# A long convolution placed beside a recurrence: one pair of heads and 128 channels at a time

## The chip, the cores and the metric

The kernel runs on one core of one Trainium2 chip. The metric is device time in microseconds (us); where several runs are shown, their median. The names in the profile: PE is TensorE (PEld its weight loads), DVE is VectorE, ACT is ScalarE, POOL is GpSimd, SP is SyncE, which here only issues transfers.

## The reference, cut to what matters

The model is two blocks. The first has an attention layer and a recurrent layer, the second another set of attention and recurrent branches and a feed-forward part. The change is in the recurrent layer of the first block, between its input product and its output product. There two branches are independent of each other: a linear recurrence of 8 heads over 256 context and 1024 latent tokens in both directions, and a long convolution of 512 channels, applied twice with a gate, by Fourier transforms of length 2048.

```python
def wkv_scan(s0, r, decay, k, v, kk, b, reverse, emit):
    def step(s, inp):
        r_t, w_t, k_t, v_t, kk_t, b_t = inp
        sa = jnp.einsum('bhij,bhj->bhi', s, kk_t)
        s = s * w_t[:, :, None, :] - sa[..., None] * b_t[:, :, None, :] + v_t[..., None] * k_t[:, :, None, :]
        y = jnp.einsum('bhij,bhj->bhi', s, r_t) if emit else None
        return s, y
    ...

def hyena_operator(u, short_taps, kern, skip):
    v, x1, x2 = split_cols(centred_conv3(u, short_taps), (HY_WIDTH, HY_WIDTH, HY_WIDTH))
    z = v
    for o, gate in enumerate((x1, x2)):
        z = gate * fft_long_conv(z, kern[:, o], skip[o])
    return z

def rec_layer(...):
    ...
    y_rw, yc_rw = rwkv_branch(u_rw, uc_rw, ...)
    y_hy = hyena_operator(u_hy, hy_short, hyena_filters(...), hy_skip)
    y = jnp.concatenate([y_rw * jax.nn.silu(g_rw), y_hy * jax.nn.silu(g_hy)], axis=-1) @ w_out
```

## The kernel before, in words

The program is written as Python generators that issue instructions; a scheduler of the tile framework then fixes the order of the instructions on each engine. At run time each engine takes its queue strictly in that order. PSUM has 8 banks; `banks(s=5, pt=2, o=1)` deals them out to tags, and `bank(tag)` goes round among the banks of a tag.

The recurrent layer's middle has these stages, one after the other:

- The input product (`rec_dense`), with the features of the recurrence and the triangular inverses (`rwkv_inverse`) of head pairs 0 and 1 and of the context as background work. An inverse is 31 rounds of a product (L1660, `ush`) and a subtraction (L1662, `r_X`).
- The convolution (`hyena`), alone. It goes through four passes, one for each order `o` and each half `hh` of 256 channels. A forward part transposes the input, multiplies it with the DFT table `F` (L1281, for each half `f` of the frequencies), and does the last butterflies and the product with the filter's spectrum `K` on VectorE (all through the helper at L1271). An inverse part multiplies the spectra `G` with the table `I` (L1338) and adds skip and gate on VectorE (L1342 and after it). `z` and `K` have two buffers, `G` three; the inverse of one pass is woven into the forward part of the next.
- The recurrence (`rwkv_chains`, `rwkv_scan`). Tokens are taken in chunks of 64: 4 chunks of context and 16 of latents, so 20 steps. A chain is one pair of heads in one direction. Four chains run at once, pairs 0 and 1 in 20 steps, then pairs 2 and 3 in 20 more. A step of a chain (`steps`): two matmuls with the state `SV` (L1789), a copy `R` on ScalarE (L1791), two matmuls (L1799), two copies into `UV`, one on ScalarE (L1800) and one on VectorE (L1801), two matmuls with `tm` (L1806), and two operations on VectorE that scale and add the state scaled before on GpSimd, `sp` (L1795), and so give the next `SV` (L1809). The output `y` (L1815, four matmuls) is copied on ScalarE (L1820) or added on VectorE (L1822). Every four steps each chain has one preparation (`prep`): `eta` on GpSimd (L1737), matmuls L1741, masks on VectorE (L1746), matmuls L1753 and the copy `tm` (L1755), copies of `SV` into `UV` (L1757), matmuls L1763 and copies `AE` (L1766), matmuls L1771 and copies `T` (L1774). Its seven loads go through SP's queue. Beside the first steps run the inverses of pairs 2 and 3, their products on GpSimd; beside steps 20 to 39 run the readouts of pairs 0 and 1.
- The output product (`rec_w_out`), which begins by splitting `yH` and `yB` on ScalarE (L406); the readouts of pairs 2 and 3 run beside its first part.

Of the kernel before, what the change touches and what calls it, by code (L numbers as in the profile page):

```python
# [11 lines left out]
F32 = mybir.dt.float32  # L12
# [1014 lines left out]
class KernB(Kern):  # L1027
# [198 lines left out]
    def hyena(self, d_hy, d_sgh, yH):  # L1226

        nc, tc, A = self.nc, self.tc, self.A
        self.banks(s=4, o=2, pt=2)
        with self.pool(name="hyF", bufs=1, side="right") as pf, self.pool(name="hy", bufs=1) as p:  # L1230
            F = self.t(pf, [128, 4, 1024], F32, "F")
            self.reserve(p, ("z", 8, 2), ("K", 8, 2), ("W1", 4, 1), ("W2", 4, 1), ("Z", 8, 1), ("T", 8, 1), ("Y", 8, 1), ("G", 8, 3))
            I = self.t(p, [128, 4, 1024], F32, "I")
            for r in range(4):
                nc.gpsimd.dma_start(yH[:, r], d_hy[r * 128:(r + 1) * 128, :])
                self.load_r(F[:, r], A["dft_f1"][r])
            inv = self.inverse_load(I)
            for o in range(2):
                for hh in range(2):
                    G = []  # L1240
                    for _ in self.hyena_fwd(p, o, hh, F, yH, G):
                        next(inv, None)
                    for _ in inv:
                        pass
                    inv = self.hyena_inv(p, o, hh, I, yH, G, d_hy, d_sgh)
            for _ in inv:
                pass
        self.banks(s=4, pt=2, o=2)

    def inverse_load(self, I):  # L1250

        for _ in range(4):
            yield
        for r in range(4):
            yield
            self.pace(self.load_r(I[:, r], self.A["dft_i1"][r]), self.mark)

    def hyena_fwd(self, p, o, hh, F, yH, Gs):

        nc = self.nc  # L1260
        z = self.t(p, [128, 8, 256], F32, "z", bufs=2)
        for cc in range(2):
            zr = yH[:, hh * 2 + cc].rearrange("p (t r) -> p r t", r=4)
            for q in range(2):
                ps = self.bank("o")
                for i in range(4):
                    j = q * 4 + i
                    nc.tensor.transpose(ps[:, i * 128:(i + 1) * 128], zr[:, j // 2, (j % 2) * 128:(j % 2) * 128 + 128], self.ident)
                nc.scalar.activation(z[:, q * 4:q * 4 + 4, cc * 128:(cc + 1) * 128], ps.rearrange("p (j c) -> p j c", c=128), AF.Copy)
                yield  # L1270
        add = lambda o, x, y, op=OP.add: nc.vector.tensor_tensor(o, x, y, op)  # L1271
        for f in range(2):
            K = self.t(p, [128, 4, 2, 256], F32, "K", bufs=2)
            nc.sync.dma_start(K.rearrange("p s c e -> p (s c e)"), self.d_spec[o, hh, f])
            X = {}
            for r in range(4):
                X[r] = self.bank("s", (128, 2, 256))
# [5 lines left out]
            E, O = (self.t(p, [128, 2, 2, 256], F32, n, bufs=1) for n in ("W1", "W2"))  # L1283
# [7 lines left out]
            Z = self.t(p, [128, 4, 2, 256], F32, "Z", bufs=1)  # L1291
# [3 lines left out]
            Y = self.t(p, [128, 4, 2, 256], F32, "Y", bufs=1)  # L1295
            T = self.t(p, [128, 4, 2, 256], F32, "T", bufs=1)
            part = lambda i: Z[:, :, i:i + 1].to_broadcast([128, 4, 2, 256])
# [11 lines left out]
            G = self.t(p, [128, 4, 2, 256], F32, "G", bufs=3)  # L1309
# [5 lines left out]
    def hyena_inv(self, p, o, hh, I, yH, Gs, d_hy, d_sgh):  # L1315

        nc = self.nc
        for cc in range(2):
            ct = hh * 2 + cc
            gate = self.t(p, [128, 1024], F32, "gate", bufs=2)  # L1320
            row = (1 + o) * 512 + ct * 128
            nc.sync.dma_start(gate, d_hy[row:row + 128, :])
            if o == 1:
                sg = self.t(p, [128, 1024], F32, "sgh", bufs=2)
                nc.sync.dma_start(sg, d_sgh[512 + ct * 128:512 + ct * 128 + 128, :])
                nc.vector.tensor_tensor(gate, gate, sg, OP.mult)
            zs = yH[:, ct]
            nc.scalar.activation(zs, zs, AF.Copy, scale=self.c("hy_skip", o * 4 + ct))
            zsr = zs.rearrange("p (t r) -> p r t", r=4)
            for rp in range(2):  # L1330
                ps = self.bank("pt", (128, 2, 256))
                for i in range(2):
                    r = rp * 2 + i
                    n = 0
                    for f in range(2):
                        for half in range(2):
# [346 lines left out]
    def rwkv_scan(self, p, R, yB, later):  # L1683
# [19 lines left out]
        for x in AEs:  # L1703
            nc.vector.memset(x, 0.0)
# [1047 lines left out]
```

## Time and profile before

| | us |
|---|---|
| median of 3 runs (lowest, highest) | 4325.55 (4324.6, 4327.83) |
| profiled execution | 4318.2 |
| its span | 4316.1 |
| its mean granted TensorE clock | 0.939 |
| busy in the span: PE | 3887.0 (90%) |
| DVE | 2779.1 (64%) |
| ACT | 1781.4 (41%) |
| POOL | 1357.6 (31%) |

The shares are averages over stages with different limits. What matters here is the stretch from 1858 us (end of the input product) to 2454 us (start of the output product). A matmul of fp32 data shows as two records, so 16 records of L1789 are one step of four chains. The clock column is the mean clock that TensorE was granted, as a share of 2.4 GHz.

### The profile page before, as it was taken

The numbers are of one execution on the slowest core, as the hardware profiler recorded it, in microseconds if no ns is written. First come the engines' busy times: TensorE is split into PE (matmuls) and PEld (weight loads), VectorE is DVE, ScalarE is ACT, GpSimd is POOL, SyncE is SP. The second block draws the span as 40 slices with busy tenths as digits, with TensorE's granted clock in tenths as the row PEclk, the third lists the DMA queues.
The fourth block names the chain that finished last, engine by engine and source line by source line (L and its number), as shares of the span: only waits on it lengthen the run. The fifth ranks groups of instructions, "written<-read, shape, count | busy, mean of one in ns | idle before, by whom it ended". The sixth has DMA issues, their size and how long they took to land.

```text
span 4316.1 us, 65300 instructions
## 1 busy us (share of the span) xinstructions
PE 3887.0 (90%) x23789; PEld 3168.0 (73%) x23789; DVE 2779.1 (64%) x5935; ACT 1781.4 (41%) x3746; POOL 1357.6 (31%) x1570
## 2 busy tenths in 40 slices
PE   7989998899999988977686888999997897999999
PEld 4768886777787767766675766777876785888787
DVE  7842426788844767759565656599777768656532
ACT  6433415777735544411453423334336523333311
POOL 5422302333324432300564334122212116554200
PEclk8899998999999999988897999999998998999999
DMA  5444326421234544531543323233336351222422
GB/s 209 151 168 164 130 75 168 122 70 31 78 109 127 184 143 135 170 144 67 134 124 107 111 65 115 93 105 116 122 105 172 105 185 58 88 79 83 151 102 74
DMA packets 351338, 511.29 MB, mean 118 GB/s; under 512 B 149864, under 2 KB 226424, under 8 KB 348329
## 3 DMA queue, kind: packets, MB, share of 16 engines
q1 hardware_dynamic: 332200, 436.33, 32.1%
q0 software_dynamic: 14064, 53.48, 3.6%
q10 hardware_dynamic: 4752, 17.30, 1.3%
q8 instruction: 188, 3.08, 0.3%
q14 instruction: 134, 1.09, 0.1%
HBM read 343.69 MB, written 164.63 MB: 118 GB/s over the span
## 4 chain that ended last, share of the span: by engine, by line
PE 37%; DVE 7%; DMA 2%; ACT 2%; issue 1%; POOL 1%; SPq 1%; ACTq 0%; DVEq 0%; POOLq 0%
PE bank L285 18%; PE bank L2493 10%; PE bank L2393 2%; DMA SV<-d_V 1%; PE bank L1741 1%; PE bank L1789 1%; PE bank L724 1%; PE bank L1815 1%; PE bank L1753 1%; PE bank L685 1%; PE bank L246 0%; DVE d L2225 0%; DVE S L694 0%; DVE SV L1809 0%; DVE junk L2225 0%
## 5 line engine op out<-in xcount | busy, mean ns | idle before, releaser
L285 PE MATMUL bank<-hhi,whi 128*128 128x512 f32 (+1 forms) x1264 | 488.6, 387 | 13.1 <-ACT hhi L399 10.1
L285 PE MATMUL bank<-hlo,whi 128*128 128x512 f32 (+1 forms) x1264 | 485.0, 384 | 4.3 <-DVE hlo L400 2.1
L285 PE MATMUL bank<-hhi,wlo 128*128 128x512 f32 (+1 forms) x1264 | 482.6, 382 | 0.0
L267 ACT ACTIVATE whi<-wf 128x1024 fp32r<-128x1024 f32 (+3 forms) x202 | 193.5, 960 | 462.1 <-PE bank L285 393.0
L268 POOL TENSOR_TENSOR wlo<-wf,whi 128x1024 fp32r<-128x1024 f32 (+1 forms) x96 | 220.5, 2298 | 462.9 <-ACT whi L267 427.8
L285 PEld LDWEIGHTS bank<-hhi,whi 128*128 128x128 f32 x1264 | 243.8, 193 | 62.7 <-ACT hhi L399 10.9
L285 PEld LDWEIGHTS bank<-hlo,whi 128*128 128x128 f32 x1264 | 243.7, 193 | 54.5 <-DVE hlo L400 4.6
L285 PEld LDWEIGHTS bank<-hhi,wlo 128*128 128x128 f32 x1264 | 242.9, 192 | 46.7
L2493 PE MATMUL bank<-th,wh 128*128 128x512 f32 x616 | 247.3, 402 | 6.8 <-ACT th L2418 6.8
L2493 PE MATMUL bank<-th,wl 128*128 128x512 f32 x616 | 246.6, 400 | 0.0
L411 POOL CAST phi<-split 128x512 fp32r<-128x512 f32 (+1 forms) x104 | 62.7, 603 | 476.4 <-ACT split L410 381.0
L322 POOL TENSOR_TENSOR walo<-wa,wahi 128x512 fp32r<-128x512 f32 x96 | 137.0, 1441 | 238.4 <-ACT wahi L321 224.0
L285 PE MATMUL bank<-yT,whi 128*128 128x512 f32 (+1 forms) x600 | 190.6, 387 | 1.1 <-ACT ush L1393 0.5
L407 DVE TENSOR_TENSOR plo<-bank,phi 128x512 fp32r<-128x512 f32 (+2 forms) x260 | 166.5, 653 | 34.9 <-ACT phi L406 32.6
L406 ACT ACTIVATE phi<-bank 128x512 fp32r<-128x512 f32 (+2 forms) x260 | 143.5, 563 | 66.7 <-PE bank L724 25.4
L1795 POOL TENSOR_SCALAR sp<-SV,PL 64x64 f32<-64x64 f32 x304 | 135.9, 448 | 80.9 <-DVE SV L1809 59.4
L285 PE MATMUL bank<-yH,whi 128*128 128x512 f32 x376 | 151.4, 403 | 7.9 <-ACT ev_a L2156 4.4
L285 PE MATMUL bank<-yB,whi 128*128 128x512 f32 x376 | 150.6, 401 | 8.0 <-DVE yB L397 7.2
L285 PE MATMUL bank<-yH,wlo 128*128 128x512 f32 x376 | 150.4, 400 | 0.0
L268 DVE TENSOR_TENSOR wlo<-wf,whi 128x1024 fp32r<-128x1024 f32 (+2 forms) x106 | 117.6, 1112 | 50.8 <-ACT whi L267 50.6
L2493 PE MATMUL bank<-tl,wh 128*128 128x512 f32 x352 | 141.8, 403 | 6.4 <-DVE tl L2419 5.2
L2493 PEld LDWEIGHTS bank<-th,wh 128*128 128x128 f32 x616 | 117.7, 191 | 36.7 <-ACT th L2418 8.7
(632 smaller groups left out, 11275.9 us busy)
## 6 DMA issues: line engine op xcount, KB each, us to landing
wf<-in_w_in_dram SPq DMA_DIRECT2D x47, 512.0 KB, 3.5
wf<-in_w_ffn_in_dram SPq DMA_DIRECT2D x44, 512.0 KB, 3.4
d_rec<-r_rec SPq DMA_DIRECT2D x40, 512.0 KB, 3.6
wf<-in_rec_w_in_dram ACTq DMA_DIRECT2D x33, 512.0 KB, 3.9
wf<-in_attn_w_in_dram SPq DMA_DIRECT2D x26, 512.0 KB, 4.3
wa<-in_attn_ada_w_dram POOLq DMA_DIRECT2D x24, 512.0 KB, 4.0
wa<-in_rec_ada_w_dram POOLq DMA_DIRECT2D x24, 512.0 KB, 4.2
LK<-d_rec SPq DMA_DIRECT2D x64, 192.0 KB, 3.3
```

The lines of the kernel that those rows point to most:

```text
L267: nc.scalar.activation(hi, wf, AF.Copy)
L268: self.wlo.tensor_tensor(lo, wf, hi, OP.subtract)
L285: self.mark = nc.tensor.matmul(ps[:, :n], w[:, k - k0, :], x(k, t0, n), start=(k == ks[0] and j == 0), stop=(k == ks[-1] and j == 2))
L322: nc.gpsimd.tensor_tensor(lo[:, k], w3[:, k], hi[:, k], OP.subtract)
L406: nc.scalar.activation(hi, src, AF.Copy)
L407: nc.vector.tensor_tensor(lo, src, hi, OP.subtract)
L411: nc.gpsimd.tensor_copy(hi, full)
L685: nc.tensor.matmul(bank[:, at:at + n], qs, kk[:, t0:t0 + n], start=(i == 0), stop=(i == 1))
L724: nc.tensor.matmul(o[:, c0:c0 + w], u["v"][:, kt, h, :], x[:, at:at + w], start=(kt == order[0] and j == 0), stop=(fin and j == 1))
L1795: nc.gpsimd.tensor_scalar(sp[half[h]], sv[half[h], h], pl[half[h]], None, OP.mult)
L2393: nc.tensor.matmul(ps, w[:, k, :], x[:, k, t0:t0 + n], start=(k == k0 and j == 0), stop=(k == k1 - 1 and j == 2))
L2493: self.mark = nc.tensor.matmul(ps, w[i][:, k, :], x[i][k], start=(k == 0 and j == 0), stop=(k == kh - 1 and j == 2))
```

## The change

The convolution becomes a generator, `beside`, that works on 128 channels in eight passes with tiles half as wide; `z` has one buffer and `G` two. It is advanced every second turn of the recurrence's loop. The recurrence runs two chains (one pair, two directions) for 80 steps instead of four for 40. In a step VectorE and GpSimd no longer take part, but for the second direction's `y`, which GpSimd adds: the state is brought into the PSUM bank by two more matmuls with the identity and scaled by ScalarE on its way into `SV`, and both halves of `UV` are ScalarE's. `UV` gets its copy of `V` by a transfer instead of L1757 (nine loads instead of seven). The masks are two operations on 64x512 instead of four on 64x256. The preparation has one PSUM bank instead of two (`pt=1`), the convolution two (`X=2`). The inverse of pair 2 moves into the background of the input product, that of pair 3 stays beside the recurrence's first 20 steps. The readouts of pairs 0, 1 and 2 run inside the recurrence, that of pair 3 beside the output product. Both DFT tables are loaded at the start.

```diff
 # hyena: eight passes, a generator
+        for r in range(4):
+            nc.gpsimd.dma_start(yH[:, r], d_hy[r * 128:(r + 1) * 128, :])
+            self.load_r(F[:, r], A["dft_f1"][r])
+        for r in range(4):
+            self.load_r(I[:, r], A["dft_i1"][r])
+        yield
+        for o in range(2):
+            for ct in range(4):
+                G = []
+                yield from self.hyena_fwd(p, o, ct, F, yH, G)
+                yield from self.hyena_inv(p, o, ct, I, yH, G, d_hy, d_sgh)
...
-        z = self.t(p, [128, 8, 256], F32, "z", bufs=2)
+        t = lambda n, *dims, bufs=1: self.t(p, [128, *dims, 128], F32, n, bufs=bufs)
+        z = t("z", 8)
...
-            Z = self.t(p, [128, 4, 2, 256], F32, "Z", bufs=1)
+            Z = t("Z", 4, 2)
             add(Z[:, 0:2], E, O)
...
-            G = self.t(p, [128, 4, 2, 256], F32, "G", bufs=3)
+            G = t("G", 4, 2, bufs=2)
...
 # rwkv_features
-                                  (None, ("s", 3, 2), [("s", i, 4) for i in range(4)])):
+                                  (None, ("s", 3, 2), [("s", i, 4) for i in range(4)]),
+                                  (2, ("s", 3, 3), [("s", 2, g) for g in range(4)] + [("i", None)])):
...
-            later = [self.rwkv_inverse(p, pair, R, 1) for pair in (2, 3)]
-            self.banks(s=5, pt=2, o=1)
-            self.rwkv_scan(p, R, yB, later)
+            self.banks(q=3, y=1, X=2, pt=1, s=1)
+            self.share["o"] = self.share["s"]
+            self.rwkv_scan(p, R, yB, self.rwkv_inverse(p, 3, R, 1), self.hyena(q, q, R["hy"], R["sg"], yH))
...
 # prep
-            p2 = [self.bank("pt", (128, 2, w, 64)) for _ in range(2)]
+            p2 = self.bank("pt", (128, 4, w, 64))
...
-            for h in range(2):
-                nc.scalar.activation(x["U"][half[1 - h], :, h], x["S"][half[1 - h], :, h], AF.Copy)
...
 # steps
-            if step < 19:
-                sp = T("sp", 4, 64)
-                for h in range(2):
-                    nc.gpsimd.tensor_scalar(sp[half[h]], sv[half[h], h], pl[half[h]], None, OP.mult)
...
-            nc.scalar.activation(uv[half[0], 0], pu[half[0]], AF.Copy)
-            nc.vector.tensor_copy(uv[half[1], 1], pu[half[1]])
-            yield
+            for h in range(2):
+                nc.scalar.activation(uv[half[h], h], pu[half[h]], AF.Copy)
             if step < 19:
-                ps = self.bank("s", (128, 64))
+                ps = self.bank("q", (128, 64))
                 for h in range(2):
-                    nc.tensor.matmul(ps[half[h]], tm[:, half[h]], uv[:, h], start=True, stop=True)
-                s1 = loaded[ch, (g + 1) // 4]["S"][:, chunk(d, step + 1) % 4]
+                    nc.tensor.matmul(ps[half[h]], self.ident[:, half[h]], sv[:, h], start=True, stop=False)
+            yield
+            if step < 19:
+                for h in range(2):
+                    nc.tensor.matmul(ps[half[h]], tm[:, half[h]], uv[:, h], start=False, stop=True)
+                s1 = loaded[d, (g + 1) // 4]["S"][:, chunk(d, step + 1) % 4]
                 for h in range(2):
-                    nc.vector.scalar_tensor_tensor(s1[half[h], h], ps[half[h]], pl[half[h]], sp[half[h]], OP.mult, OP.add)
+                    nc.scalar.activation(s1[half[h], h], ps[half[h]], AF.Copy, scale=pl[half[h]])
...
-                if (d == 0) == (c < 8):
-                    nc.scalar.activation(ysl, py, AF.Copy)
-                else:
-                    nc.vector.tensor_tensor(ysl, ysl, py, OP.add)
+                first = (d == 0) == (c < 8)
+                y = ysl if first else T("yt", 4, 64)
+                nc.scalar.activation(y, py, AF.Copy)
+                if not first:
+                    nc.gpsimd.tensor_tensor(ysl, ysl, y, OP.add)
...
 # the loop
-        for g in range(40):
+        for g in range(80):
...
+                turns += 1
...
+                if g < 20 and turns % 2:
+                    next(later, None)
+                if slow and n % 2 and next(slow[0], 0) is not None:
                     slow.pop(0)
+                if turns % 2:
+                    next(beside, None)
...
-            ro = [self.rwkv_readout(q, pair, R, yB, str(pair)) for pair in (2, 3)]
+            ro = [self.rwkv_readout(q, pair, R, yB, str(pair)) for pair in (3,)]
```

What this does to TensorE's queue, in the second half of the recurrence before, where four chains (their banks differ) share it with the preparations:

```order
L1806 MATMUL bank_5330_23372<-UV_5127_22412,tm_5234_22933 64x64 [waits DVE_49,Activation_49]
L1753 MATMUL bank_5332_23382<-ident_66,be_23028 64x64 [waits DVE_49,PE_49]
L1753 MATMUL bank_5332_23382<-ident_66,be_23028 64x64 x12
L1806 MATMUL bank_5330_23372<-UV_5127_22412,tm_5234_22933 64x64 [waits DVE_49]
L1806 MATMUL bank_5331_23377<-UV_5130_22422,tm_5240_22992 64x64 [waits Activation_49]
L1806 MATMUL bank_5331_23377<-UV_5130_22422,tm_5240_22992 64x64 [waits DVE_49]
L1753 MATMUL bank_5332_23382<-ident_66,be_23028 64x64 x3
L239 MATMUL bank_5335_23406<-identr_68,bc_c_5334_23403 16x128
L1763 MATMUL bank_5337_23410<-T_4549_19345 64x32 [waits DVE_49,PE_49]
L1763 MATMUL bank_5337_23410<-T_4549_19345 64x32 x7
```

And in the convolution's inverse part after (L1325 is the inverse DFT, L1775 the matmul with the state that was L1789, L1781 was L1799, L1787 the new one with the identity, L1791 was L1806, L1800 the output):

```order
L1775 MATMUL bank_4519_19403<-SV_4445_18953,LK_4407_18733 64x64 [waits Activation_49] x2
L1325 MATMUL bank_4796_20908<-I_18768,G_20433 128x256 [waits DVE_49]
L1781 MATMUL bank_4521_19420<-R_19401,T_4403_18724 64x64 [waits Activation_49]
L1781 MATMUL bank_4521_19420<-R_19401,T_4403_18724 64x64
L1787 MATMUL bank_4522_19425<-SV_4442_18941,ident_66 64x64 [waits PE_49]
L1787 MATMUL bank_4522_19425<-SV_4442_18941,ident_66 64x64
L1325 MATMUL bank_4796_20908<-I_18768,G_20433 128x256
L1800 MATMUL bank_4529_19479<-LK_4402_18723,SV_4442_18941 64x64 [waits Activation_49]
L1800 MATMUL bank_4529_19479<-LK_4402_18723,SV_4442_18941 64x64
L1781 MATMUL bank_4523_19428<-R_19406,T_4408_18734 64x64 [waits Activation_49]
L1781 MATMUL bank_4523_19428<-R_19406,T_4408_18734 64x64
L1791 MATMUL bank_4522_19425<-UV_4443_18942,tm_4471_19109 64x64 [waits Activation_49]
```

Each operation of the two chains now stands behind single matmuls of the convolution, and the first of these waits for VectorE.

ScalarE's queue in the second half before, where L1791, L1800 are the step's and L1755, L1766, L1774 the preparation's:

```order
L1791 ACTIVATE R_22040<-bank_5059_22037 128x64 [waits PE_49,Activation_49]
L1766 ACTIVATE AE_4564_19375<-bank_5081_22154 32x4x32 [waits PE_49]
L1766 ACTIVATE AE_4564_19375<-bank_5081_22154 32x4x32
L1800 ACTIVATE UV_4860_21082<-bank_5066_22058 64x64 [waits PE_49]
L1791 ACTIVATE R_22048<-bank_5062_22045 128x64 [waits PE_49,Activation_49]
L1800 ACTIVATE UV_4857_21072<-bank_5065_22053 64x64 [waits PE_49]
L1800 ACTIVATE UV_4863_21092<-bank_5067_22063 64x64 [waits PE_49]
L1774 ACTIVATE T_4549_19345<-bank_5094_22197 32x4x32 [waits PE_49]
```

And after, late in the recurrence, when the convolution is done (L1794 writes the state, L1806 the output, L1777 `R`, L1783 `UV`, L1744 `tm`):

```order
L1794 ACTIVATE SV_4825_21079<-bank_4915_21534,PL_13562 64x64 [waits PE_49]
L1794 ACTIVATE SV_4825_21079<-bank_4915_21534,PL_13562 64x64
L1794 ACTIVATE SV_4828_21091<-bank_4917_21542,PL_13562 64x64 [waits PE_49]
L1794 ACTIVATE SV_4828_21091<-bank_4917_21542,PL_13562 64x64
L1806 ACTIVATE yB_18710<-bank_4918_21558 128x64 [waits PE_49]
L1777 ACTIVATE R_21573<-bank_4920_21570 128x64 [waits PE_49,Activation_49]
L1777 ACTIVATE R_21578<-bank_4922_21575 128x64 [waits PE_49]
L1806 ACTIVATE yB_18710<-bank_4919_21564 128x64 [waits PE_49]
L1783 ACTIVATE UV_4826_21080<-bank_4928_21598 64x64 [waits PE_49]
L1783 ACTIVATE UV_4826_21080<-bank_4928_21598 64x64
L1744 ACTIVATE tm_4934_21650<-bank_4933_21633 128x512 [waits PE_49]
L1783 ACTIVATE UV_4829_21092<-bank_4930_21606 64x64 [waits PE_49]
```

All operations between two matmuls of a step are now ScalarE's, and the writes of the state stand in the same queue as those of the other chain and of the preparation.

## Rows read from the trace of the kernel before

**Rows 1.** Windows: length, each engine's busy us and instructions, clock, DMA, GB/s.
```profile
core 0: us, PE busy (x) PEld busy (x) DVE busy (x) ACT busy (x) POOL busy (x), PEclk, DMA share, GB/s
1872.00:2054.00 182.00, 136.03 (x544) 112.13 (x544) 160.95 (x164) 19.02 (x30) 13.12 (x14) 0.83 0.24 87
2064.00:2247.00 183.00, 146.73 (x3284) 134.46 (x3286) 108.08 (x389) 89.70 (x358) 109.29 (x252) 0.88 0.50 128
2247.00:2312.00 65.00, 33.56 (x577) 29.51 (x573) 30.41 (x105) 16.54 (x56) 25.70 (x54) 0.71 0.37 97
2312.00:2446.00 134.00, 117.69 (x2298) 102.62 (x2296) 89.06 (x327) 66.72 (x278) 67.79 (x149) 0.94 0.33 89
2438.85:2443.36 4.51, 4.51 (x73) 3.50 (x73) 3.58 (x16) 1.44 (x8) 3.52 (x8) 1.00 0.02 5
```

**Rows 2.** The same windows, matmuls of L1789 alone (PE, weight loads).
```profile
2064.00:2247.00 183.00, 37.94 (x332) 27.73 (x332) 0.88 0.50 128
2247.00:2312.00 65.00, 4.33 (x48) 2.98 (x48) 0.71 0.37 97
2312.00:2446.00 134.00, 27.11 (x264) 17.99 (x260) 0.94 0.33 89
```

**Rows 3.** VectorE by line and form, 1850 to 2053: busy us, mean ns, idle before.
```profile
L1271 DVE TENSOR_TENSOR Z<-W,W 128x1024 f32<-128x1024 f32 x16 | 18.9, 1227 | 0.2
...
L1271 DVE TENSOR_TENSOR Z<-Y 128x512 f32<-128x512 f32 x8 | 5.5, 690 | 0.0
```

**Rows 4.** ScalarE by line and form, 2053 to 2454.
```profile
L1791 ACT ACTIVATE R<-bank 128x64 f32<-128x64 f32 x160 | 30.8, 222 | 47.6 <-PE bank L1789 41.1 <-PE bank L1753 3.8 <-PE bank L1799 1.5
...
L1800 ACT ACTIVATE UV<-bank 64x64 f32<-64x64 f32 x160 | 28.2, 213 | 20.4 <-PE bank L1799 18.1 <-PE bank L1789 0.7
...
L1755 ACT ACTIVATE tm<-bank 128x512 f32<-128x512 f32 x40 | 23.7, 594 | 11.0 <-PE bank L1753 8.3 <-PE bank L1806 2.3
...
L1766 ACT ACTIVATE AE<-bank 32x128 f32<-32x128 f32 x80 | 21.5, 269 | 12.1 <-PE bank L1763 9.3 <-PE bank L1789 0.5 <-PE bank L1806 0.2
```

**Rows 5.** GpSimd by line and form, 2053 to 2454.
```profile
L1795 POOL TENSOR_SCALAR sp<-SV,PL 64x64 f32<-64x64 f32 x304 | 135.9, 448 | 80.9 <-DVE SV L1809 59.4
L1737 POOL COPY eta<-be 64x256 f32<-64x256 f32 x80 | 31.8, 398 | 50.8 <-DMA be<-d_rec 33.8 <-PE bank L1771 6.6 <-PE bank L1799 3.1
```

**Rows 6.** Timeline of TensorE: start, us, records, idle before and its releaser.
```profile
1903.25 1.89 PE L1338 MATMUL bank<-I,G 128*128 128x256 f32 x8
...
2405.72 0.61 PE L1763 MATMUL bank<-T 128*64 128x32 f32 x16
...
2410.32 0.66 PE L1741 MATMUL bank<-LK,eta 128*64 128x128 f32 x8 [0.18 <-ACT T L1774]
...
2430.66 0.78 PE L1753 MATMUL bank<-ident,be 128*64 128x64 f32 x20
...
2434.71 0.29 PE L1799 MATMUL bank<-R,T 128*64 128x64 f32 x4
...
2436.80 0.51 PE L1799 MATMUL bank<-R,T 128*64 128x64 f32 x10
...
2437.39 0.34 PE L1799 MATMUL bank<-R,T 128*64 128x64 f32 x4
```

**Rows 7.** Timeline of TensorE, where a readout's matmuls stand between those of a preparation.
```profile
2360.18 1.05 PE L1874 MATMUL bank<-sel,yB 128*128 128x2 f32 x8
2361.17 0.98 PE L1741 MATMUL bank<-LK,eta 128*64 128x128 f32 x11
```

**Rows 8.** Timeline of GpSimd, 2225 to 2320.
```profile
2291.41 0.25 POOL L1660 TENSOR_TENSOR ush<-r_X,r_U 128x31 f32<-128x31 f32 x1 [0.34 <-DVE r_X L1662]
...
2311.29 4.01 POOL L1795 TENSOR_SCALAR sp<-SV,PL 64x64 f32<-64x64 f32 x8 [19.63 <-DVE SV L1809]
```

**Rows 9.** Timeline of TensorE, first DFT matmuls.
```profile
1872.20 15.69 PE L1281 MATMUL bank<-z,F 128*128 128x256 f32 x64 [0.56 <-DMA F<-in_dft_f_dram]
```

**Rows 10.** Timeline of ScalarE, first work of the output product.
```profile
2453.76 2.95 ACT L406 ACTIVATE yhi<-yH 128x1024 fp32r<-128x1024 f32 x3 [6.75 <-PE bank L1815]
```

More of the change, by code (lines that the diff above doesn't have):

```diff
@@ L1223, in fwd_butterfly @@
         nc.vector.tensor_tensor(sp[:, 3], d, y, OP.subtract)
[L1226 to L1233, printed above, removed]
-            for r in range(4):
[L1235 to L1248, printed above, removed]
@@ new lines, in hyena_inv @@
+        gate = self.t(p, [128, 1024], F32, "gate", bufs=1)
+        row = (1 + o) * 512 + ct * 128
+        nc.sync.dma_start(gate, d_hy[row:row + 128, :])
+        if o == 1:
+            sg = self.t(p, [128, 1024], F32, "sgh", bufs=1)
+            nc.sync.dma_start(sg, d_sgh[512 + ct * 128:512 + ct * 128 + 128, :])
+        zs = yH[:, ct]
+        nc.scalar.activation(zs, zs, AF.Copy, scale=self.c("hy_skip", o * 4 + ct))
+        zsr = zs.rearrange("p (t r) -> p r t", r=4)
+        for rp in range(2):
+            ps = self.bank("X", (128, 2, 256))
+            for i in range(2):
+                r = rp * 2 + i
+                n = 0
+                for f in range(2):
+                    for half in range(2):
+                        kt = half * 2 + f
+                        nc.tensor.matmul(ps[:, i, :], Gs[f][:, r, half], I[:, r, kt * 256:(kt + 1) * 256], start=(n == 0), stop=(n == 3))
+                        n += 1
+                    yield
+            nc.vector.scalar_tensor_tensor(zsr[:, rp * 2:rp * 2 + 2, :], ps, self.rn[:, o, ct:ct + 1],
+                                           zsr[:, rp * 2:rp * 2 + 2, :], OP.mult, OP.add)
@@ L1775, in prep, with steps @@
             yield
-        def steps(ch, g):
-            pi, d = ch
-            pair, step = g // 20 * 2 + pi, g % 20
+        def steps(d, g):
+            pair, step = divmod(g, 20)
             c = chunk(d, step)
-            i, x = c % 4, loaded[ch, g // 4]
+            i, x = c % 4, loaded[d, g // 4]
             LK, tm, sv, uv = x["LK"], x["tm"][:, i], x["S"][:, i], x["U"][:, i]
@@ L1818, in steps @@
                     ysl = ysl[:, ::-1]
-                if (d == 0) == (c < 8):
-                    nc.scalar.activation(ysl, py, AF.Copy)
-                else:
-                    nc.vector.tensor_tensor(ysl, ysl, py, OP.add)
-        for ch in chains:
-            load(ch, 0)
-        for ch in chains:
-            for _ in prep(ch, 0):
-                pass
-        slow, preps = [], []
-        for g in range(40):
-            if g % 4 == 0 and g < 36:
-                for ch in chains:
-                    load(ch, g // 4 + 1)
-                preps = [prep(ch, g // 4 + 1) for ch in chains]
-            if g == 20:
-                assert not later
-                slow = [self.rwkv_readout(p, pair, R, yB) for pair in range(2)]
-            gens = [steps(ch, g) for ch in chains]
+                first = (d == 0) == (c < 8)
[3 more added lines that the diff above has]
+                    nc.gpsimd.tensor_tensor(ysl, ysl, y, OP.add)
+        for d in range(2):
+            load(d, 0)
+        next(beside)
+        for d in range(2):
+            for _ in prep(d, 0):
+                next(beside, None)
+        slow, preps = [], []
+        turns = 0
+        for g in range(80):
+            if g % 4 == 0 and g < 76:
+                for d in range(2):
+                    load(d, g // 4 + 1)
+                preps = [prep(d, g // 4 + 1) for d in range(2)]
+            if g % 20 == 0 and g:
+                assert next(later, 1) == 1 and not slow
+                slow = [self.rwkv_readout(p, g // 20 - 1, R, yB)]
+            gens = [steps(d, g) for d in range(2)]
             n = 0
@@ L1842, in rwkv_scan @@
                 n += 1
+                turns += 1
                 if preps and g % 4 and next(preps[0], 0) is not None:
                     preps.pop(0)
-                if later and next(later[0], 0) is not None:
-                    later.pop(0)
-                if slow and n % 4 and next(slow[0], 0) is not None:
+                if g < 20 and turns % 2:
+                    next(later, None)
+                if slow and n % 2 and next(slow[0], 0) is not None:
                     slow.pop(0)
+                if turns % 2:
+                    next(beside, None)
+        for _ in beside:
+            pass
         assert not slow
```

162 lines of the change are left out of this document (69 added, 93 removed).

## Prediction

> **What bounds the kernel now.** I read the profile in this order: the page for the busy shares, the windows for the stage that the change touches, the groups by line for what an operation costs there, and the timeline for rates and gaps. The stretch runs from the end of the input product at 1858 us to the first work of the output product at 2453.76 [rows 10]. Everything outside it I take to stay as it is.
>
> In the convolution, 1872 to 2054, VectorE is busy 160.95 of 182 us and TensorE 136.03, while ScalarE has 19.02 and GpSimd 13.12 [rows 1]. VectorE ends that stage; the other two are nearly free. The recurrence is the opposite case: no engine is full. From 2064 to 2247 TensorE is busy 146.73 of 183 us, VectorE 108.08, GpSimd 109.29, ScalarE 89.70, and from 2312 to 2446 it is 117.69 of 134, with VectorE at 89.06 [rows 1]. Sixteen records of L1789 are one step of four chains, so 332 records are 20.75 steps at 8.8 us, and 264 are 16.5 steps at 8.1 us; between them 65 us hold only 48 records, three steps [rows 2]. That hole is the inverse of pair 3, which the second half needs: GpSimd's last product of it begins at 2291.41, and its first state product of the new pairs comes after an idle time of 19.63 us [rows 8]. The granted clock is 0.71 of 2.4 GHz there, and 0.83 in the convolution [rows 1], so both stages leave TensorE idle. An undisturbed step of four chains lasts 4.51 us, with eight VectorE and eight GpSimd operations filling 3.58 and 3.52 of it [rows 1].
>
> So the gain on offer is the overlap of a stage that VectorE limits with one that waits, plus the hole. The price is that two chains instead of four have to hide each other's waits, with the convolution's instructions in the same queues.
>
> **The change part by part.** The new stage has a part B, in which the convolution runs, and a part C after it. In the order of the changed kernel the last DFT matmul lies at step 47 of 80, so B is 48 steps and C is 32.
>
> *VectorE in B.* Halving the tiles doubles the 136 operations of the helper. A 128x1024 one takes 1227 ns and a 128x512 one 690 [rows 3], so two halves cost 153 ns more than a whole: 136 × 0.153 = 21 us on top of 160.95, 182 in all. The 24 preparations of B have two masks each, of 512 columns; at the 690 ns of that width this is 33 us. The 31 subtractions of pair 3's inverse are at most 31 × 0.69 = 21. Together about 236 us. The recurrence's own share is gone from VectorE.
>
> *TensorE in B.* Eight DFT records of 256 columns take 1.89 us, 0.236 each [rows 6]. The inverse has 256 of these (60 us), the forward part 512 records of 128 columns, at half the price another 60, and with 64 transposes of 128 columns, taken at the same price, that is 127 us. Four records of a step take 0.29 us and ten take 0.51 [rows 6], so one more costs 0.037, and about 0.14 is a tail that the next may overlap. A chain's step has 12 matmuls, two of them new (the identity), so 24 records: 96 chain-steps are 2304 records, 85 us without gaps. A preparation has 16 records like those at 0.61 twice, 16 of 128 columns (eight in 0.66) and 32 like the twenty in 0.78 [rows 6]; less the tails that is 0.47 × 2 + 1.04 + 1.02 = 3.0 us, and 24 of them 72. The floor is 127 + 85 + 72 = 284. In PE's queue of the changed kernel 238 times a matmul of the convolution's form stands next to one of the recurrence's form. Two such neighbours in the trace overlap by 0.06 us only (2360.18 + 1.05 against 2361.17) [rows 7], where the tail within a form is 0.14. I charge 0.08 for each, 19 us, which makes the floor 303.
>
> The Trainium skill, "TensorEngine Tiling (Array Packing)", § Key Properties, says that changing the tiling mode drains the engine, which speaks against this change. The rows agree, with a price of 0.08 us; without any drain both ends of B would be 19 us lower, and so would my sum; with a drain of a whole 0.2 us they and the sum would be 29 us higher.
>
> For a ceiling I take the pace that the recurrence really had: 134 us for 2298 records, 0.0583 each, gaps, waits and readouts included [rows 1]. B has 2304 + 24 × 80 = 4224 records of the recurrence: 246 us, plus the convolution's own 136.03 as busy when alone, plus 19: 401. I take the middle of 303 and 401, 350 us. VectorE would then be busy 67%, less than it was.
>
> *Part C.* ScalarE has per chain-step `R` 0.222, two `UV` of 0.213, two writes of the state that I price like them, and `y` at 0.222: 1.30, or 2.6 for two chains. A preparation is 0.594 + 4 × 0.269 = 1.67, and there is half of one per step, 0.83 [rows 4]. The floor is 3.43 us for a step. From the other side, a step of two chains has 48 + 40 = 88 records, 5.1 us at 0.0583. The state product on GpSimd (448 ns, 304 times) goes away, `eta` (398 ns) stays [rows 5], so GpSimd limits nothing. Middle: 4.3 us, times 32 is 138.
>
> *The single bank of the preparation* puts its four parts, and those of both chains, in one line. Its TensorE work is 3.0 us and its ScalarE work 1.67, with masks of 1.4 and `eta` of 0.8 about 6.9; two of them in four steps are 3.5 us per step, under B's 7.3 and C's 4.3. I charge nothing; if the waits between the parts cost 1 us more per part, it would be 5.4 per step, and C, not B, would grow by 35 us.
>
> *Start and tail.* The first DFT matmul began at 1872.20, waiting for the table [rows 9]. The tables now stand behind memsets on GpSimd; I take 1880, bounds 1872 and 1890. From the last `y` to the output product ScalarE idles 6.75 us [rows 10]; I take 8.
>
> *The rest at nothing.* Pair 2's inverse in the input product's background lies beside a stage that TensorE's matmuls fill, and no step before g = 40 reads it; if it ran over the end it would be at most one inverse's tail, some 8 us by 31 × 0.25. One readout less beside the output product: 0, for the matmuls there cover it. Two more loads for each preparation: 0, since they are issued four steps early; if SP's queue fell behind, both chains would stop at the first read of `UV`. The hole goes, since pair 3 is needed only at step 60.
>
> *Sum.* 1880 + 350 + 138 + 8 = 2376, where the output product began at 2453.76: 78 us less. 4318.2 − 78 = 4240; the median lies 7.35 above the profiled execution, so 4248.
>
> **The rivals.**
>
> Better overlap (15%): B at the floor without drains, 284, and C at ScalarE's floor, 110. 1880 + 284 + 110 + 8 = 2282, 172 less: 4154. For it: VectorE held 88% in the convolution, and TensorE 100% of the undisturbed step [rows 1]. Against it: in no long stretch of the recurrence did any engine hold that.
>
> The queues add instead of overlapping (15%): the convolution's matmuls wait for VectorE at the head of TensorE's queue, and the recurrence stands behind them. Then it is 182 + 21 for the convolution, the 10 us that lay between the stages, 80 × 4.3 = 344 and 8, from 1872: 2437, 17 less, 4309. The change would not do what it says, and only the hole and the wider sharing would be paid back. For it: after the change single DFT matmuls that wait for VectorE stand between the steps. Against it: the convolution then has its operands a pass ahead only in part, but it needs just one wait per 16 matmuls.
>
> The slower side (15%): a step is bound by its chain of waits, not by work. Then two chains need as long as four did, and the stage has twice as many steps. Three hops from TensorE to ScalarE and back, each behind a preparation or DFT matmuls in both queues, at 7.5 us for a step make 1890 + 600 + 8 = 2498, 44 more: 4370. It decides from (2453.76 − 8 − 1890) / 80 = 6.95 us on; at the 8.1 of before it would be 2546, 4418. For it: 8.1 us for a step [rows 2] with no engine full. Against it: the undisturbed step of four chains took 4.51 us, and one chain came from L1799 at 2434.71 to L1799 at 2437.39 [rows 6], 2.7 us for a whole round.
>
> **How the numbers follow.** The forecast has 55% and its own range is 4190 to 4300: B between 303 and 390, C between 3.5 and 5 us a step. The rivals have 15% each. The range of 4155 to 4335 leaves out half of the better overlap and most of the slower side. A difference of 0.2%, 8.6 us, is about what a measurement of this kernel can tell from none. Faster: 0.55 + 0.15 + 0.11 of the adding queues = 0.81. Same: 0.05, between the adding queues and the slow steps. Slower: 0.14.
>
> **What would show it.** In the profile after: the output product's first split near 2376; TensorE's busy share over 85% from 1880 to 2230, at a granted clock over 0.9; VectorE about 240 us busy there; the last inverse DFT matmul near 2230; then steps at 4.3 us, with ScalarE at 75% or more; no hole before the last pairs. If matmuls of the convolution wait long for VectorE while both chains' copies are done, the queues add. If a step takes over 7 us with every engine under 70%, the waits bind, and the prediction is wrong. If the input product ends later than 1858, the moved inverse has a price.

## The result and the profile after

The changed kernel takes 4264.16 us (4257.82 to 4265.35, 4 runs) against 4326.28 (4324.6 to 4327.83): a ratio of 0.9854 with a 95% interval of 0.9836 to 0.9871, 63 us less by the ratio. The forecast was 4248, so the sign, the range and the forecast's own range hold, and it promised 16 us too much. The profiled execution took 4263.1 us, with a span of 4261.3.

First the windows of the kernel after, with the convolution and behind it; the columns are those of [rows 1].

```profile
core 0: us, PE busy (x) PEld busy (x) DVE busy (x) ACT busy (x) POOL busy (x), PEclk, DMA share, GB/s
1874.00:2234.00 360.00, 319.94 (x4728) 278.59 (x4730) 230.68 (x436) 189.12 (x694) 78.94 (x135) 0.94 0.51 140
2234.00:2407.00 173.00, 152.60 (x3004) 135.19 (x3000) 40.52 (x96) 130.22 (x520) 26.74 (x67) 0.94 0.37 98
```

TensorE is busy 319.94 of 360 us (89%) at a clock of 0.94, where the convolution alone had 136.03 of 182 at 0.83 [rows 1]. VectorE's 230.68 us are the 236 that were summed up, and its share is down to 64%. The matmul with the state, L1775, counts the steps (8 records are one step of two chains):

```profile
core 0: us, PE busy (x) PEld busy (x), PEclk, DMA share, GB/s
1891.00:2234.00 343.00, 33.65 (x358) 22.92 (x357) 0.95 0.48 131
2234.00:2407.00 173.00, 29.02 (x280) 20.27 (x280) 0.94 0.37 98
2280.00:2312.00 32.00, 6.62 (x64) 4.69 (x64) 1.00 0.46 118
2331.00:2376.00 45.00, 7.09 (x64) 4.93 (x64) 0.89 0.37 98
```

The first window has 358 records, 45 steps in 343 us, 7.7 us a step. The second has 35 steps in 173 us, 4.94 a step. Within it the pace differs: 8 steps in the 32 us of the third window, 4.0 a step, and 8 in the 45 us of the fourth, 5.6. Pair 2's readout runs beside most of the fourth, and the granted clock is 0.89 there against 1.00 in the third. All engines in these two:

```profile
2280.00:2312.00 32.00, 29.66 (x680) 26.43 (x679) 4.44 (x8) 26.73 (x109) 7.46 (x24) 1.00 0.46 118
2331.00:2376.00 45.00, 39.54 (x760) 35.59 (x756) 11.64 (x29) 31.84 (x127) 5.72 (x12) 0.89 0.37 98
```

TensorE is the busiest in both, 93% and 88%; ScalarE is busy 26.73 of 32 us, 3.3 a step. The convolution's last group of inverse DFT matmuls (the last record of it begins at 2233.4) and the first split of the output product (TensorE, then ScalarE):

```profile
2230.90 2.86 PE L1325 MATMUL bank<-I,G 128*128 128x256 f32 x12
```
```profile
2406.89 0.22 ACT L1806 ACTIVATE yt<-bank 128x64 f32<-128x64 f32 x1 [0.61 <-PE bank L1800]
2407.55 2.00 ACT L406 ACTIVATE yhi<-yH 128x1024 fp32r<-128x1024 f32 x2 [0.43 <-POOL yB L1808]
```

The split began at 2453.76 before [rows 10], so 46 us of the span's 55 were won in this stretch. The other 9 lie behind it, but the stretch from that split to the end differs by as much between kernels that have the same work there (1853.1 to 1861.2 us with one readout beside the output product, 1859.4 to 1864.5 with two), so that only some 4 us, the difference of the means of these runs, can be put to the readout. ScalarE's largest groups in the steps after the convolution, by line and form:

```profile
L1794 ACT ACTIVATE SV<-bank,PL 64x64 f32<-64x64 f32 x120 | 37.1, 309 | 6.3 <-PE bank L1791 3.6
...
L1783 ACT ACTIVATE UV<-bank 64x64 f32<-64x64 f32 x128 | 27.8, 217 | 16.1 <-PE bank L1731 11.7 <-PE bank L1781 1.5
```

`UV` costs what it did [rows 4]; the write of the state, which scales by a column of `PL`, takes 309 ns, not the 213 that it was priced at.

### The profile page after: what moved, and what is told of

It is laid out like the page before. It is cut to its first block, busy times and chain, and to the rows that moved or that the text cites. A ratio compares the mean times of both kernels' runs of the same rounds, so it can differ in the third digit from the quotient of the medians.

```text
span 4261.3 us, 66864 instructions
## 1 busy us (share of the span) xinstructions
PE 3897.0 (91%) x24653; PEld 3178.8 (75%) x24653; DVE 2670.2 (63%) x5484; ACT 1896.8 (45%) x4210; POOL 1250.0 (29%) x1299
## 5 line engine op out<-in xcount | busy, mean ns | idle before, releaser
L698 ACT ACTIVATE P<-S,mx 128x768 f32<-128x768 f32 (+7 forms) x144 | 117.4, 816 | 63.6 <-DVE mx L694 56.9
```

The source lines that it names most:

```text
L698: nc.scalar.activation(P[:, :at], S[:, :at], AF.Exp, bias=m[:, i:i + 1], scale=-1.0, accum_out=st["rs"][:, bi, u["h"]:u["h"] + 1])
```

## The experiments

Each kernel is compared by its ratio to the kernel before, measured beside it; the changed kernel's ratio is 0.9854. The stretches in the rows are those of one profiled execution.

**The convolution ahead of the steps.** The first state is made from the last row that the convolution writes.

```diff
-        next(beside)
+        for _ in beside:
+            pass
...
-                    nc.gpsimd.memset(sv[half[h], h], 0.0)
+                    if g == 0:
+                        nc.gpsimd.tensor_scalar(sv[half[h], h], yH[half[h], 3, 0:64], 0.0, None, OP.mult)
+                    else:
+                        nc.gpsimd.memset(sv[half[h], h], 0.0)
```

> The changed kernel, but the first state of the first pair is made from the last row that the convolution writes, times zero, so that no step begins before the convolution's end (its order in the queues then has all 384 DFT matmuls ahead of the first step). Overlap theory (the gain is the convolution beside the steps): the convolution alone takes 200 to 230 us from 1874 with the narrow tiles, then 80 steps at 4.4 to 4.7 us, the output product begins near 2455 to 2470 instead of 2407.5: 4310 to 4330 us. Rival (the queues add; the gain is the recurrence on two chains and the lost hole): within 15 us of the changed kernel, 4264 to 4280.

Measured: 4415.97 us, ratio 1.0203 (1.0186 to 1.022), 152 us more than the changed kernel and 85 more than before. Against the same narrow convolution laid apart, the overlap is worth more than twice the whole gain, and the rival of adding queues falls. The windows of this kernel show why it is so much: the convolution, then the steps.

```profile
1874.00:2170.00 296.00, 182.62 (x1146) 155.70 (x1146) 194.40 (x340) 34.64 (x74) 32.11 (x51) 0.77 0.30 88
2170.00:2540.00 370.00, 328.01 (x6492) 288.57 (x6491) 78.12 (x191) 280.23 (x1114) 55.40 (x147) 0.94 0.43 112
```

Alone, the narrow convolution needs 296 us, not the 200 to 230 expected: VectorE works 194 of them. Who waits for whom, 1900 to 2150:

```profile
PE bank L1325 <- DVE G L1256: 72.3, 13, 8.0
...
PEld bank L1325 <- DVE G L1256: 45.9, 8, 8.2
```

TensorE waits for `G`, the end of VectorE's work in the same pass. The kernel before wove one pass's inverse part into the next forward part and held VectorE at 88%. That one `z` and eight passes in a row are what prevents this here is argued from the code, not tested. Alone, with pair 3's inverse beside it, the narrow convolution takes 114 us more than the wide one; it pays only because the steps fill the gaps.

**No convolution.** The loop over its passes is left out, its loads stay.

```diff
-        for o in range(2):
+        for o in range(0):
```

> The changed kernel without the convolution (its tables and inputs are loaded, its passes are left out). Overlap theory: the steps go at the 4.5 to 4.8 us of the part after the convolution, 80 of them from 1885 to about 2255, 150 us less: 4105 to 4125 us. Rival (the queues add): the whole 203 us of the convolution go, 4061. Rival (a step is bound by its chain of waits, whatever else is in the queues): steps at 6.5 us as beside the convolution, less than 40 us go.

Measured: 4167.26 us, ratio 0.9625 (0.961 to 0.964). Beside the steps the convolution costs about 0.023 of 4326, some 99 us, where it had 182 of its own. The recurrence alone, from its first `R` to the split 414 us:

```profile
1887.00:2301.00 414.00, 350.09 (x6849) 309.26 (x6849) 93.57 (x229) 293.58 (x1160) 77.04 (x193) 0.90 0.45 115
2000.00:2298.00 298.00, 268.22 (x5362) 236.63 (x5358) 70.35 (x179) 230.72 (x917) 48.61 (x126) 0.95 0.44 115
```
```profile
2000.00:2298.00 298.00, 52.22 (x503) 35.71 (x503) 0.95 0.44 115
```

In the second window its pace is 4.7 us (the last row is L1775 in it: 503 records, 63 steps in 298 us), the theory's figure. The first eight steps are slow without the convolution too: the last of their 64 records of L1775 ends at 1959.7, and at 1964.1 in the changed kernel, some 73 us after the first `R` in both. From 1890 to 1925 TensorE is busy 20.27 of 35 us at a clock of 0.55, and from 1890 to 1960 its longest waits, 15.6 us in four times, are for the masks, which stand in VectorE's queue between the subtractions of pair 3's inverse. So the convolution runs for nothing beside these steps. At 4.7 us they would take 38, so this is 35 of the 51 us by which the gain falls short of 150.

```profile
1890.00:1925.00 35.00, 20.27 (x271) 17.80 (x271) 7.53 (x19) 10.89 (x41) 11.06 (x24) 0.55 0.42 92
```
```profile
PE bank L1742 <- DVE LK L1735: 15.6, 4, 6.6
```

**The hole alone.** The kernel before with pair 2's inverse in the input product's background, and nothing else.

```diff
+                                  (2, ("s", 3, 3), [("s", 2, g) for g in range(4)] + [("i", None)])):
...
-            later = [self.rwkv_inverse(p, pair, R, 1) for pair in (2, 3)]
+            later = [self.rwkv_inverse(p, pair, R, 1) for pair in (3,)]
```

> The kernel before, with one part of the change: pair 2's inverse in the background of the input product, so that only pair 3's runs beside the first 20 steps. Theory (the hole of 65 us with three steps was this work, and the product's stage hides it): 30 to 45 us less than before, 4281 to 4296, and no hole between the halves. Rival (the hole is made of the loads and preparations of the new pairs, or the input product ends later): within 10 us of before.

Measured: 4286.29 us, ratio 0.99 (0.9885 to 0.9915), 43 us less than before. The window in which the kernel before did three steps of L1789 [rows 2], in this kernel, where the line is L1790:

```profile
2242.00:2312.00 70.00, 12.11 (x132) 8.21 (x132) 0.93 0.50 133
```

132 records, more than eight steps, in 70 us, against 48 records in 65. So two thirds of the change's gain is this one part of it, and everything else together (the overlap, two chains for four, ScalarE's and the identity's part) brings the remaining 20 us. The recurrence on four chains then lasts from 2075 to the split at 2416.28, 341 us; on two chains, without the convolution, 414. The change pays 73 us in the recurrence for the overlap. The row of this kernel, to be laid beside that of the kernel without the convolution:

```profile
2075.00:2416.00 341.00, 289.81 (x6176) 262.78 (x6175) 218.07 (x796) 169.28 (x689) 182.36 (x411) 0.91 0.44 115
```

By its records TensorE is busy 289.81 us here and 350.09 there, with 673 records fewer here. So 60 of the 73 us are time in which TensorE works (the matmuls with the identity and pair 2's readout are among the added records), and only 13 are time in which it waits.

**TensorE's time beside the convolution.** One of four terms of the inverse DFT is kept, three are left out.

```diff
+                        if n == 3:
-                        nc.tensor.matmul(..., start=(n == 0), stop=(n == 3))
+                            nc.tensor.matmul(..., start=True, stop=True)
```

> The changed kernel with one of four terms of the inverse DFT only: 96 of 128 matmuls left out, about 45 us of TensorE's time in the convolution's stretch, everything else unchanged. Theory (TensorE's time sets that stretch, where it is busy 92%): 30 to 45 us less, 4220 to 4234. Rival (the chain of the convolution's passes through VectorE sets it): under 12 us less.

Measured: 4221.34 us, ratio 0.9759 (0.9744 to 0.9775): 41 us less than the changed kernel, nearly all of the 45 us at which the left-out matmuls were priced.

**VectorE's time beside the convolution.** The second spectrum product and its two sums are left out.

```diff
-            add(T, part(1), K[:, :, ::-1], OP.mult)
-            yield
-            add(Y[:, :, 0], Y[:, :, 0], T[:, :, 0], OP.subtract)
-            add(Y[:, :, 1], Y[:, :, 1], T[:, :, 1])
+            yield
```

> The changed kernel without the second product with the spectrum and the two sums that use it (48 operations on VectorE, 42 us at 1.27 and 0.72 us each); TensorE's work is the same. Theory (TensorE's time sets the stretch beside the convolution): under 12 us less, 4252 to 4266. Rival (the chain of the passes through VectorE): 25 to 42 us less.

Measured: 4252.09 us, ratio 0.9837 (0.9815 to 0.9859), 7 us less with the intervals overlapping, a sixth of what about the same amount of work brings on TensorE. From the first `R` to the split, in the changed kernel, with a quarter of the inverse, and in this kernel:

```profile
1891.60:2407.50 515.90, 459.79 (x7625) 401.94 (x7624) 267.40 (x522) 318.26 (x1211) 102.61 (x193) 0.95 0.44 120
1885.60:2362.70 477.10, 425.85 (x7433) 375.92 (x7432) 268.38 (x522) 318.99 (x1211) 103.23 (x193) 0.94 0.48 129
1885.20:2386.80 501.60, 450.19 (x7623) 392.12 (x7622) 233.56 (x475) 319.37 (x1211) 90.95 (x193) 0.98 0.47 124
```

With a quarter of the inverse the stretch is 39 us shorter and TensorE is busy 34 us less. Here VectorE is busy 34 us less and the stretch is 14 us shorter, but it ran at a clock of 0.98 against 0.95, and TensorE was busy 10 us less for the same work; some 5 us are left for VectorE. The order changed too: 36 steps, not 45, lie before the last inverse matmul. So TensorE's time sets most of the stretch; that VectorE's sets nothing of it is not shown.

**What sets the 4.9 us after the convolution.** Four edits each take one suspect away; `late` is from step 46 or 48 on.

```diff
 # state on VectorE, late
+                    if g >= 46:
+                        nc.vector.tensor_scalar(s1[half[h], h], ps[half[h]], pl[half[h]], None, OP.mult)
 # three banks for the preparation, late
+            if g == 48:
+                ...
+                self.share["pt"] = [self.share["pt"][0] + self.share["X"][0], 0]
 # no identity matmuls, late: sp on GpSimd, added on VectorE, as before
+                        nc.vector.scalar_tensor_tensor(s1[half[h], h], ps[half[h]], pl[half[h]], sp[half[h]], OP.mult, OP.add)
 # the second half of UV and of the state on VectorE, late
+                if h and g >= 46:
+                    nc.vector.tensor_copy(uv[half[h], h], pu[half[h]])
```

> The changed kernel, with the write of the state on VectorE instead of ScalarE from step 46 on, when the convolution is done (two operations of about 0.28 us per chain-step). Theory (ScalarE sets the pace there: 3.83 us of work in a step of 4.7): 34 steps get 0.4 to 0.6 us shorter, 14 to 20 us less than the changed kernel, 4244 to 4250. Rival (TensorE or the waits for the single bank set it): within 5 us of the changed kernel.

> The changed kernel, but from step 48 on the preparation goes round among three banks, its own and the convolution's two. Theory (after the convolution a step's 4.7 us is TensorE's queue with its tails, 88 records at 0.053): within 6 us of the changed kernel, 4258 to 4270. Rival (the four parts of both preparations wait for their one bank; the last four steps, which have no preparation, take 3.3 us): 32 steps get 0.6 to 1.0 us shorter, 4232 to 4245.

> The changed kernel with the state's update of the kernel before from step 46 on: scaled on GpSimd, added on VectorE, without the two identity matmuls (8 of 88 records of a step). Theory (TensorE's records set the pace after the convolution): 34 steps get 0.3 to 0.45 us shorter, 10 to 15 us less, 4249 to 4254. Rival (the chain of hops sets it): within 5 us, or slower by GpSimd's 0.45 us in the chain.

> The changed kernel, but from step 46 on the second head's half of UV and of the state is written by VectorE, at the same time as ScalarE writes the first. Theory (after the convolution a step is set by its chain, three hops with 1.27 us of ScalarE in a row, while TensorE and ScalarE each stand close behind): the chain gets 0.5 us shorter and ScalarE 1.05 us freer, 34 steps get 0.3 to 0.5 us shorter, 4247 to 4254. Rival (TensorE's records set it): within 5 us.

Measured: 4264.49 us and 0.9849 (0.983 to 0.9869) with the state on VectorE; 4272.73 and 0.9884 (0.9866 to 0.9902) with three banks; 4276.42 and 0.9893 (0.9876 to 0.9909) without the identity; 4276.71 and 0.9889 (0.9875 to 0.9904) with the split. None is faster; by the ratio the last three are slower by 13 to 17 us, three banks with an interval that overlaps the changed kernel's. From the last inverse matmul to the split the changed kernel takes 174.1 us, with 3008 records on TensorE; the four kernels in the order above:

```profile
2234.60:2409.40 174.80, 149.53 (x3008) 133.05 (x3006) 76.41 (x224) 92.03 (x392) 26.79 (x68) 0.92 0.37 98
2236.00:2408.80 172.80, 151.98 (x3008) 133.76 (x3006) 40.54 (x96) 131.56 (x520) 27.42 (x70) 0.96 0.38 100
2229.30:2413.90 184.60, 156.53 (x2752) 138.98 (x2750) 76.20 (x224) 91.12 (x392) 82.80 (x196) 0.83 0.35 92
2233.20:2408.30 175.10, 147.96 (x3008) 131.31 (x3006) 72.02 (x228) 88.52 (x388) 26.93 (x68) 0.94 0.38 98
```

ScalarE's busy time falls from 130 us to 92 and 88 in the first and the last, and the stretch stays: ScalarE is not the limit, nor is the chain that the last one shortens, and three banks change nothing. The 13 and 15 us of three banks and of the split are not in this stretch; where they arise is not known. Without the identity the stretch is 10 us longer, but the granted clock was 0.83 there against 0.94, so this run can't tell what 256 records less are worth. What is left is TensorE, busy 153 of the 174 us in the changed kernel; the rows are on its side, but no run shows it. Whether the loads, all issued by SP, have a part wasn't tried; TensorE's longest wait from 2256 to 2406 is for them, 6.4 us in all.

**The readout.**

```diff
-                slow = [self.rwkv_readout(p, g // 20 - 1, R, yB)]
+                slow = [self.rwkv_readout(p, g // 20 - 1, R, yB)] if g < 60 else []
...
-            ro = [... for pair in (3,)]
+            ro = [... for pair in (2, 3)]
```

> The changed kernel with pair 2's readout beside the output product again, as in the kernel before, instead of beside steps 60 to 79. Theory (a readout costs about 9 us beside the output product, which is the difference of the two kernels after the split of yH, and as much or more beside the steps): the end of the steps comes 10 to 20 us earlier, the output product takes 9 us longer: 4254 to 4264. Rival (beside the steps a readout is free): the end of the steps stays, 4270 to 4276.

Measured: 4257.01 us, ratio 0.9845 (0.983 to 0.986), not told apart from the changed kernel as a whole. The matmuls with the state in steps 60 to 79, from the first of them to the split, in the changed kernel and in this one:

```profile
2311.00:2407.50 96.50, 16.99 (x160) 11.67 (x160) 0.95 0.36 95
2299.10:2385.60 86.50, 17.11 (x160) 11.40 (x160) 1.00 0.40 106
```

The twenty steps are 10 us shorter without the readout. The clock differs too, 1.00 against 0.95, so the 10 us are the readout's price and the clock's together, and the two are not separated. Behind the split this kernel takes 1859.4 us and the changed one 1853.8, so that about half comes back there, within what kernels with the same work differ by.

**VectorE in every step.** The split of the fourth edit above, in all 80 steps.

> The same split in all 80 steps. Theory: beside the convolution TensorE's time sets the pace, so nothing more is won there, and VectorE's 1 us in each step, some 45 us on top of 231, delays the convolution's passes a little: the same as with the split in the late steps, 4245 to 4260. Rival (the chain sets the pace there too): 20 us less than with the late split, under 4235.

Measured: 4320.46 us, ratio 0.9984 (0.997 to 0.9997), 56 us slower than the changed kernel: both expectations fail. The convolution's last inverse matmul begins at 2244.8, 11 us later than in the changed kernel, and only 35 steps lie before it in TensorE's order instead of 45. TensorE's waits from 1900 to 2240 now have a row that the changed kernel has not:

```profile
PE bank L1775 <- DVE SV L1798: 10.6, 8, 3.0
```

and ScalarE waits 55.6 us for L1794, the matmuls with `tm`, where the same wait takes 25.9 us in the changed kernel:

```profile
ACT SV L1800 <- PE bank L1794: 55.6, 25, 6.5
```

A step's half on VectorE can stand behind the convolution's operations of 0.7 to 1.3 us. Ten steps more behind the convolution at 4.9 us each are most of the 56 us. The scheduler's order and the waits changed together, and no run separates them; but with one half of a step on VectorE nearly the whole gain of the change is lost.

**The convolution spread over the steps.** Each pass after the first begins with a copy of the current state into `z`, and three turns of four advance it.

```diff
+        if o or ct:
+            nc.gpsimd.tensor_copy(z[0:64, 0, 0:64], self.state)
...
-                if turns % 2:
+                if turns % 4:
```

> The changed kernel with the convolution spread over the steps: each pass after the first begins with a copy of the recurrence's state into its z, so that it can't be ordered before the step at which it is issued, and it is advanced in three turns of four; its last DFT matmul then lies at step 75 instead of 45. Theory (45 steps are bound by TensorE and 35 by their chain, so work moved from the first to the second costs little): a step takes 6.2 to 6.4 us throughout, the last ends near 2390, 4240 to 4255. Rival (a step beside the convolution loses by the form changes and waits in the queue, not by TensorE's time): 80 steps at 6.8 us or more, 4290 or slower.

Measured: 4260.77 us, ratio 0.9854 (0.984 to 0.9869): no difference, between theory and rival. The last inverse matmul begins at 2381.7 instead of 2233.4. From the first `R` to the split:

```profile
1891.70:2402.50 510.80, 465.48 (x7625) 406.32 (x7625) 271.26 (x522) 318.02 (x1211) 99.18 (x200) 0.94 0.46 121
```

TensorE is busy 465 us, as in the changed kernel (460), and the stretch is within 5 us of it. Where the convolution's work lies doesn't matter, which fits a limit that is TensorE's in both parts. No kernel here with all of the work beats the changed one beyond its interval.

## Why the prediction was right, point by point

- *Part B, 350 us.* The end is right: the last group of inverse matmuls began at 2230.9, forecast near 2230, and TensorE's time sets most of it (41 us came back for the 45 left out). VectorE's 236 us were 231. The price of a form change, 0.08 us, is borne out by the rows at the end of this document; no run shows what all of them cost together. But I took 48 steps from the queue and it was 45: the first eight took 73 us beside pair 3's inverse, with or without the convolution, which the sum did not have. That the end still fell at 2230 is in part luck. Three steps of 4.9 us, 15 us, were left for C.
- *Part C, 4.3 us a step.* This is the term that was mis-sized: 4.94 measured, 20 us over 32 steps. The floor lacked the 309 ns of the state's write, 0.38 us a step, but that moves the middle by 0.19 only, 6 of the 20 us. The step that failed is taking the middle. The upper bound, TensorE's pace of 0.0583 us a record, was nearly right: 3004 records in 173 us are 0.0576, at the same clock of 0.94. ScalarE's floor counted for nothing, for with ScalarE relieved C stayed as long.
- *The tail, 8 us.* It was 0.4: the last `y` is followed at once by the split, since the convolution's rows are ready. With the 4 us of B's end these terms make 4 + 15 + 20 − 8 = 31 us, the split at 2407.55 instead of 2376.
- *Luck in the total.* The stretch thus won 46 us where 78 were forecast, but the time is only 16 us off. The work behind the split was 9 us shorter in the profiled execution, by as much as kernels with the same work differ there, and the median lay 1 us above the profiled execution, not 7.35. The forecast had neither.
- *The hole.* Right, and larger than its place in the text: 43 of 63 us. I had counted it inside the paces and not priced it by itself, so the sum didn't say how little the rest brings.
- *Rivals.* The adding queues are refuted by 152 us. Better overlap failed at both floors. The slower side failed: 4.7 us a step alone, far from 6.95. The recurrence on two chains did lose 73 us to four, but 60 of them are TensorE's work and not the waits that this rival names.
- *Costed at nothing.* The single bank held: more banks brought nothing. Pair 2's inverse was free: with it alone the input product's last matmul begins at 1855.04, before at 1854.29. The readout beside the output product is worth a few us.

## What to carry to other kernels

Before two stages are merged, take out of the profile what can be had without merging: here one hole gave two thirds of the gain. A stage that is laid beside another need not be fast alone. Look also at what the other stage puts on the first one's limiting engine: here one half of each step on VectorE cost 56 of the 63 us. Work taken off an engine that does not set the pace brings nothing, even if that engine stands close behind: 40 us less on ScalarE changed nothing. When two bounds lie far apart, ask which of them was measured with all the waits in it, instead of taking the middle.

## What the runs showed of the hardware

A ScalarE copy of 64x64 from PSUM with a scale from a column took 309 ns in the changed kernel, and without one 217 ns. In the narrow convolution alone, VectorE worked 194 of 296 us and TensorE was granted a mean clock of 0.77; beside the steps it was 0.94, and the same 256 inverse DFT records took 68.6 us of TensorE instead of 91.4:

```profile
L1325 PE MATMUL bank<-I,G 128*128 128x256 f32 x256 | 91.4, 533 | 82.4 <-DVE G L1256 82.4
```
```profile
L1325 PE MATMUL bank<-I,G 128*128 128x256 f32 x256 | 68.6, 411 | 5.0 <-DVE G L1256 5.0
```

The first row is the kernel with the convolution apart, the second the changed one. The better clock is a part of what the overlap is worth; how large a part wasn't measured.

Where the matmul's form changes on TensorE, some 0.08 us of overlap are lost, as here in the changed kernel:

```profile
2227.15 2.86 PE L1325 MATMUL bank<-I,G 128*128 128x256 f32 x12
2229.94 0.66 PE L1750 MATMUL bank<-T 128*64 128x32 f32 x16
```

The matmul of the other form begins 0.07 us before the twelve end. Within the twelve, at 0.379 us each in 2.86 us, one overlaps the next by 0.15.
